# Gated delta rule: whole 128x128 products in the scan, and q's norm taken out of the products

## Chip, cores and metric

One core of a Trainium2 chip runs the whole program. The metric is the device time of one execution in microseconds (us): the median of several runs. One execution is also recorded by the hardware profiler, and every row below is from that record.

## What is computed

A network of two blocks of two layers each on 512 tokens of 1024 features, in float32. The change touches one part alone, the mixer of the second layer of the first block, a gated delta rule with 8 heads of 128. Its reference, cut to what matters:

```python
qkv = silu(causal_depthwise_conv(proj[..., :3 * 1024], conv_w))     # 4 taps
q = l2norm(q) * 128 ** -0.5;  k = l2norm(k)
decay = exp(where(incl, g[..., :, None] - g[..., None, :], -inf))   # chunks of 64 tokens
lower = where(strict, einsum('cd,sd->cs', k * beta, k) * decay, 0)
u, w  = solve(lower + eye, [v * beta, k * beta * exp(g)])
attn  = einsum('cd,sd->cs', q, k) * decay
def step(state, ...):                                                # 8 chunks, one after the other
    v_new = u_c - w_c @ state
    o     = (q_c * exp(g_c)) @ state + attn_c @ v_new
    state = state * exp(g_last) + (k_c * exp(g_last - g_c)).T @ v_new
o = rmsnorm(o, norm_g) * silu(z)
```

## The kernel before

The mixer is the method `gdn` (L811). A large product (L243 to L245) is done three times, in exact high and low parts, with 128 weight rows and 512 tokens each; it is called background below where it fills time between other steps. Per head there are these steps.

- `gdn_pre` (L948): the convolutions of k, q and v (`gdn_conv`, L909: a projection on TensorE, a copy by ScalarE, four taps on VectorE, a silu on ScalarE). k and then q are normed: squares on ScalarE, their sums by four products (L338), a power on GpSimd (L352), for q a factor on VectorE (L958), four transposes on TensorE that spread the result over the rows (L359), and a multiplication on VectorE into the tile `qk` (L960). Then the products of k with k and with q (L965), times the decay, give `U` and `at` (L969, L972); `wq`, `bk`, `kd` and `u` are prepared.
- `gdn_inverse` (L1000): a triangular inverse, first as a long chain of short VectorE instructions (L1016 to L1018), then as products on TensorE (L1027) with copies in between; it ends with the copies into `u` and `wq` (L1066).
- `gdn_scan` (L1068): eight steps in a chain, one for each chunk of 64 tokens. Two chunks share a tile of 128 partitions, and chunk e of a tile lies on partitions 64e to 64e+63. A step is a product of the state `S` with `wq` (L1079, 128 rows, 128 columns), a subtraction on VectorE into `vn` (L1082, 64 partitions), the product `at` by `vn` (L1083, 64 rows and 64 columns), the product `kd` by `vn` (L1087, 64 rows and 128 columns; not in the last step), the new `S` on VectorE (L1088) and a copy of the output by ScalarE (L1090). A float32 product is issued as two passes, so each counts twice in the rows.
- `gdn_out` (L1092): the norm of the output over its 128 features (squares, a sum, a factor and epsilon, L1098 and L1099, a power on GpSimd, L1101, a multiplication, L1102), four transposes, the gate and the split into parts. `out_proj` follows for pairs of heads.

The loop of `gdn` writes head after head: three heads' `gdn_pre` ahead, then for each head its scan, the inverse of the head after the next, `gdn_pre` of the third one on, the gate rows and the output. Heads 6 and 7 are scanned together at the end. The order on each engine is made from this program by a list scheduler when the kernel is built, from priorities and assumed durations; on the chip each engine takes its instructions in that order. So background products of later heads stand between the steps of a scan on TensorE.

Of the kernel before, what the change touches and what calls it, by code (L numbers as in the profile page):

```python
# [9 lines left out]
F32 = mybir.dt.float32  # L10
# [19 lines left out]
# ------------------------------------------------------------------ constants  # L30

class Pack:
    """Columns of a [128, n] array, by name."""
# [15 lines left out]
def shape_constants():  # L49
    """Arrays that depend on shapes alone: identity, masks, rope tables."""  # L50
# [4 lines left out]
    # causal mask, q on partitions  # L55
    c.add("causal", np.where(col <= row, 0.0, NEG))
    # stick-breaking, k on partitions and q along the free axis; the first 128
    # columns are the queries before the diagonal block
# [3 lines left out]
    # partial rope: per-row inverse frequency and sign of the sine  # L62
# [4 lines left out]
    # gated delta rule: 64-token chunks, two to a 128-token tile  # L67
# [10 lines left out]
    # axial rope, signed sines; dims 64 and 32  # L78
# [9 lines left out]
    # window attention: the blocks before and after the query's  # L88
# [6 lines left out]
def vector_packs(v):  # L95
    """Small vectors, features along partitions (layout only); the second pack
    is needed in the second block alone."""
# [18 lines left out]
# ------------------------------------------------------------------ kernel  # L116

# of the steps between the heads of a unit, the share spread evenly; the rest follows them
SPEED = 0.6
# of the convolutions, by unit: the stream that ends, the one that starts, steps of it;  # L120
# last, the steps before the first unit
CONV0 = (("", "", 3), ("", "", 3), ("c", "x", 4), ("", "", 8), ("x", "", 0), ("", "", 0), 4)
CONV1 = (("", "", 4), ("", "", 2), ("", "", 0), ("", "", 0), ("x", "", 0), ("", "", 0), 6)
# weights loaded ahead of the steps that take them
AHEAD = 2
# groups whose weights times values are float32 products, to spare the split
WHOLE_A, WHOLE_C, WHOLE_D = False, True, False
# background steps per product of 512 tokens with [1024, 128]; such products per pair of heads
# [4 lines left out]
class Step:  # L133
    """Something to do, and the (chunk, column) of the weights that it takes."""
# [5 lines left out]
class Net:  # L140
# [5 lines left out]
    # ---- small helpers  # L146
# [21 lines left out]
    def split(self, hi, lo, src, scale=None):  # L168
        """hi + lo = src exactly, hi with 12 significant bits."""
        nc = self.nc  # L170
        if scale is None:
            nc.scalar.copy(hi, src)  # L172
            nc.vector.tensor_sub(lo, src, hi.bitcast(F32))  # L173
        else:
            nc.scalar.mul(hi, src, scale)
            nc.vector.scalar_tensor_tensor(lo, src, scale, hi.bitcast(F32),
                                           op0=ALU.mult, op1=ALU.subtract)

    def exp_and_ln(self, after):
        """the activation tables that hold both, once `after` is there"""  # L180
# [4 lines left out]
    def tick(self, work):  # L185
        """background steps, so many per product of 512 tokens with [1024, 128]"""
# [11 lines left out]
    # ---- weights  # L198
    def wchunk(self, src, cut="col"):
        """Rows k*128.., columns -> get(k, c0, m): the exact (hi, lo) parts of a  # L200
        block. Loaded and split in units of 1024 when first used: all rows of
        some columns, or half of the rows."""
# [22 lines left out]
    def load_ahead(self, *uses):  # L225
        """steps that load weights, (src, column[, row, cut]) each, before their phase"""
# [12 lines left out]
    def mm3(self, out, terms):  # L239
        """out = sum of lhs^T rhs, each operand as (hi, lo)."""  # L240
# [6 lines left out]
    def mm_fm(self, out, w, c0, h, kt=KD, m=P):  # L247
        """Features on partitions: out[m, tokens]. The first ones after a norm go
        in two halves of the tokens, as these become ready."""
# [7 lines left out]
    def mm_tm(self, out, w, c0, n, h, t, kt=KD):  # L257
        """Tokens on partitions: out[128 tokens, n features]."""
# [3 lines left out]
    def t2(self, tag, n=T, dtype=F32, rows=P):  # L262
        """A short-lived [rows, n] tile, n <= 512. Tiles of one tag are given
        out in the order of the program, so steps of a chain have their own."""
# [6 lines left out]
    def psum_pool(self, **banks):  # L271
        """The half of PSUM that a phase cuts up for itself, into tags of so many
        banks (s: pairs of banks); the other half is dn and tp in all phases."""
# [13 lines left out]
    # ---- conditioning vectors  # L287
    def ada_tasks(self, w, groups, conds, dsts, bias, bufs=3, bank="st", on_pe=()):
        """conds[i] @ w + bias into dsts[i] ([128, 48], column j: features 128j..),
        as a list of steps of a quarter MB of weights each; on_pe: of the halves  # L290
        of groups, those that the tensor engine sums."""
# [34 lines left out]
    def gain_scale(self, dst, g, mod, grp):  # L326
        """dst = g * (1 + scale)"""
# [3 lines left out]
    # ---- norms  # L331
    def rstd_cols(self, acc, n, mat, scale=1.0, tag="rs"):
        """acc [128, n tokens] (sums of squares per partition), mat the averaging
        matrix (over scale) -> rstd per token, tokens on partitions [128, n/128]."""
# [7 lines left out]
    def rstd(self, means, nt, scale=1.0, tag="rs"):  # L342
        """(means scale + eps)^-1/2; scale: a number, or columns"""
# [11 lines left out]
    def bcast_rows(self, r, nt):  # L355
        """[128, nt] per-token values -> [128, nt*128] on all partitions (PSUM)."""
# [5 lines left out]
    def mean_squares(self, w, x, weights):  # L362
        """sums over the features of x^2 times weights(k) [128, j]: tokens on partitions, [128, n/128, j]"""
# [18 lines left out]
    def modulated(self, w, x, rb, A, B, hh, hl):  # L382
        """hh + hl = x * rb * A + B"""
# [12 lines left out]
    def norm_work(self):  # L396
        """short-lived tiles of a norm of 256 tokens: n and m one each, others in turn"""
# [12 lines left out]
    def hnorm(self, x, n, A, B, pool=None, size=256):  # L410
        """h = x * rstd * A + B in exact parts, and the steps that make it, two
        for `size` tokens: their norms, and the rest."""
# [21 lines left out]
    def normed_residual(self, x, n, g, A=None, B=None):  # L434
        """Steps, two for 256 tokens, for x = x * rstd * g in place; and, for A
# [1472 lines left out]
```

## Time and profile before

| | |
|---|---|
| runs | 3471.39 us median of 3 (3466.99 to 3474.49) |
| profiled execution, span from first to last instruction | 3467.6 us |
| mean granted TensorE clock | 0.980 |
| TensorE busy in the span | 3301.1 us (95%) |
| VectorE busy | 2207.0 us (64%) |
| ScalarE busy | 1274.4 us (37%) |
| GpSimd busy | 98.7 us (3%) |
| the delta rule's stage | from about 778 us to 1199 us of the span |

For the profiled execution the span is what is recorded; the time of a run also holds what lies before its first and after its last instruction, and the median of the runs is 3.8 us above that span. Products are pipelined, and the duration shown for one overlaps the next, so what a product costs TensorE is read from the distances between starts.

### The profile page before, as it was taken

Reading aid. Unit: us, or ns where it says so; the run is one execution under the profiler, and the core shown is the slowest. Engines: PE = TensorE matmul, PEld = TensorE weight load, DVE = VectorE, ACT = ScalarE, POOL = GpSimd, SP = SyncE. Lnnn points to the kernel's source line nnn. Section 1 sums busy time; section 2 is a strip of 40 time slices with the busy share of each in tenths; the row PEclk is TensorE's granted clock in tenths of the full one; section 3 lists DMA queues with packets and bytes.
Section 4 is the critical chain, followed back from the end, with each engine's and each line's share of the span. In section 5 each row is a group of like instructions: output and inputs, shape, how many; then the busy total and the mean of one; then the engine's idle time right before and its main releaser. Section 6 shows DMA issues by size and latency. Waiting matters only on the chain.

```text
span 3467.6 us, 47045 instructions
## 1 busy us (share of the span) xinstructions
PE 3301.1 (95%) x17888; PEld 2698.8 (78%) x17888; DVE 2207.0 (64%) x4501; ACT 1274.4 (37%) x2467; POOL 98.7 (3%) x122
## 2 busy tenths in 40 slices
PE   7998999999999999999899989999999898989999
PEld 4886888877777687887777768888888776778886
DVE  6977655568877576666777876543444976753334
ACT  3566322234433232223554453212122555442222
POOL 4000000000000000000000000000000000000000
PEclk9999999999999999999999999999999999989999
DMA  7554455532111155553443322333332443413332
GB/s 227 169 141 149 125 166 168 160 99 56 43 43 49 39 165 152 164 156 104 120 131 89 109 83 77 110 109 116 110 110 64 122 135 103 120 48 98 97 92 79
DMA packets 480082, 389.78 MB, mean 112 GB/s; under 512 B 21360, under 2 KB 390128, under 8 KB 479856
## 3 DMA queue, kind: packets, MB, share of 16 engines
q1 hardware_dynamic: 479856, 386.77, 37.4%
q8 instruction: 141, 2.31, 0.3%
q14 instruction: 85, 0.70, 0.1%
HBM read 356.28 MB, written 17.83 MB: 108 GB/s over the span
## 4 chain that ended last, share of the span: by engine, by line
PE 43%; DVE 4%; ACT 3%; issue 1%; DMA 1%; POOL 0%; SPq 0%; POOLq 0%; DVEq 0%; ACTq 0%
PE dn L243 6%; PE dn L244 6%; PE dn L245 6%; PE d L243 6%; PE d L245 6%; PE d L244 6%; PE tp L1181 1%; PE s L1217 1%; PE tp L1200 1%; PE tp L1207 1%; ACT pr L1160 1%; DVE cv L1346 1%; DVE wlo L173 1%; PE dn L370 1%; DVE st L1157 0%
## 5 line engine op out<-in xcount | busy, mean ns | idle before, releaser
L172 ACT CAST whi<-raw 128x1024 fp32r<-128x1024 f32 (+1 forms) x399 | 417.1, 1046 | 785.9 <-PE d L245 429.6
L173 DVE TENSOR_TENSOR wlo<-raw,whi 128x1024 fp32r<-128x1024 f32 (+1 forms) x399 | 486.5, 1220 | 284.0 <-ACT whi L172 283.7
L243 PE MATMUL dn<-hh,whi 128*128 128x512 f32 (+1 forms) x1688 | 620.8, 369 | 9.9 <-ACT t2b L1331 4.7
L244 PE MATMUL dn<-hh,wlo 128*128 128x512 f32 (+1 forms) x1688 | 614.6, 365 | 0.0
L245 PE MATMUL dn<-hl,whi 128*128 128x512 f32 (+1 forms) x1688 | 612.8, 364 | 0.0
L243 PE MATMUL d<-hh,whi 128*128 128x512 f32 (+1 forms) x1120 | 400.7, 358 | 0.0
L244 PE MATMUL d<-hh,wlo 128*128 128x512 f32 (+1 forms) x1120 | 399.9, 357 | 0.0
L245 PE MATMUL d<-hl,whi 128*128 128x512 f32 (+1 forms) x1120 | 399.8, 357 | 0.0
L243 PEld LDWEIGHTS dn<-hh,whi 128*128 128x128 f32 x1688 | 321.4, 191 | 60.6 <-ACT t2b L1331 5.3
L245 PEld LDWEIGHTS dn<-hl,whi 128*128 128x128 f32 x1688 | 320.8, 190 | 47.5 <-issue 2.9
L244 PEld LDWEIGHTS dn<-hh,wlo 128*128 128x128 f32 x1688 | 321.7, 191 | 43.8 <-issue 1.6
L310 DVE SCALAR_TENSOR_TENSOR acc<-araw,cond,acc 128x512 f32<-128x512 f32 x322 | 241.9, 751 | 67.1 <-DMA araw<-in_ada_w 39.0
L243 PE MATMUL d<-gh,whi 128*128 128x512 f32 (+1 forms) x696 | 251.6, 362 | 0.0
L244 PE MATMUL d<-gh,wlo 128*128 128x512 f32 (+1 forms) x696 | 249.9, 360 | 0.0
L245 PE MATMUL d<-gl,whi 128*128 128x512 f32 (+1 forms) x696 | 248.7, 360 | 0.0
L243 PEld LDWEIGHTS d<-hh,whi 128*128 128x128 f32 x1120 | 210.7, 188 | 32.6 <-issue 1.3
L244 PEld LDWEIGHTS d<-hh,wlo 128*128 128x128 f32 x1120 | 210.8, 188 | 32.5 <-issue 1.3
L245 PEld LDWEIGHTS d<-hl,whi 128*128 128x128 f32 x1120 | 210.7, 188 | 31.5 <-DVE hl L390 0.9
L243 PEld LDWEIGHTS d<-gh,whi 128*128 128x128 f32 x696 | 130.6, 188 | 26.4 <-issue 3.1
L245 PEld LDWEIGHTS d<-gl,whi 128*128 128x128 f32 x696 | 130.1, 188 | 24.6 <-issue 2.6
L244 PEld LDWEIGHTS d<-gh,wlo 128*128 128x128 f32 x696 | 130.6, 188 | 23.7 <-issue 2.2
L507 DVE TENSOR_TENSOR t2b<-t2a,d 128x512 f32<-128x512 f32 (+1 forms) x67 | 42.0, 627 | 154.4 <-PE d L245 154.3
(493 smaller groups left out, 5666.3 us busy)
## 6 DMA issues: line engine op xcount, KB each, us to landing
araw<-in_ada_w SPq DMA_DIRECT2D x192, 256.0 KB, 3.8
araw<-in_w_ada SPq DMA_DIRECT2D x192, 256.0 KB, 3.0
raw<-in_ffn_w_in SPq DMA_DIRECT2D x88, 512.0 KB, 4.0
raw<-in_ffn_w_out SPq DMA_DIRECT2D x44, 512.0 KB, 4.3
raw<-in_w_in SPq DMA_DIRECT2D x44, 512.0 KB, 3.9
raw<-in_w_gate SPq DMA_DIRECT2D x44, 512.0 KB, 3.7
raw<-in_w_up SPq DMA_DIRECT2D x44, 512.0 KB, 3.7
raw<-in_w_down SPq DMA_DIRECT2D x44, 512.0 KB, 3.8
```

What stands on the lines that cost most here:

```text
L172: nc.scalar.copy(hi, src)
L173: nc.vector.tensor_sub(lo, src, hi.bitcast(F32))
L243: self.nc.tensor.matmul(out, lhsT=lh, rhs=rh, start=j == 0, stop=False)
L244: self.nc.tensor.matmul(out, lhsT=ll, rhs=rh, start=False, stop=False)
L245: self.nc.tensor.matmul(out, lhsT=lh, rhs=rl, start=False, stop=j == n - 1)
L310: nc.vector.scalar_tensor_tensor(st[i], raw, s, st[i], op0=ALU.mult, op1=ALU.add)
L370: nc.tensor.matmul(sums, lhsT=weights(k), rhs=sq, start=k == 0, stop=k == KD - 1)
L507: nc.vector.tensor_mul(y, s, pu[:, :n])
L1160: nc.scalar.activation(pr, s, AF.Exp, bias=st[:, 0:1], accum_out=st[:, 2:3])
L1181: nc.tensor.transpose(tp[:, n * P:(n + 1) * P], pr[:, c:c + P], self.ident)
L1200: nc.tensor.matmul(ps[:64, q0:q1], lhsT=lhs, rhs=pt[sl // 2][0][:, sl % 2, q0:q1].bitcast(F32), start=j == 0, stop=j == nb - 1, skip_group ...
L1207: nc.tensor.matmul(ps[:, q0:q1], lhsT=lhs, rhs=pt[sl // 2][i][:, sl % 2, q0:q1], start=j == 0 and i == 0, stop=j == nb - 1 and i == 1, ski ...
```

## The change

The products `at` by `vn` and `kd` by `vn` take all 128 rows. For that `vn` has four fixed tiles, two for each half of the partitions, in which the other half is set to zero once, at the start; the subtraction still writes 64 partitions. The product with `at` also takes 128 columns: the tile `at_` has 64 more columns on either side, set to zero by GpSimd, and a window of 128 columns is chosen so that the chunk's 64 fall on the right half of the output; the other 64 add into rows of the bank that nobody reads afterwards. q is no longer normed ahead of the products: silu writes q straight into `qk`, and the norm's factor, one per token, is kept as `rq` and applied to the output at its norm: the mean square is multiplied by rq squared, and the result of the power by rq. The transposes and the multiplication that spread q's norm over the rows are gone. Comments are also left out of the file.

```diff
@@ gdn
+            self.vn = [[gp.tile([P, P], F32, name=f"vn{e}{i}") for i in range(2)] for e in range(2)]
+            self.vn_turn = [0, 0]
+            for tiles in self.vn:
+                for t in tiles:
+                    nc.gpsimd.memset(t, 0.0)
@@ gdn_conv(self, gp, w_in, tile_no, h, dst=None)
-        nc.scalar.activation(acc, acc, AF.Silu)
-        return acc
+        out = acc if dst is None else dst
+        nc.scalar.activation(out, acc if dst is None else acc.rearrange("p (t c) -> p t c", c=P), AF.Silu)
+        return out
@@ gdn_pre
-        for j in (1, 0):
-            q = self.gdn_conv(gp, w_in, j * 8 + hd, h)
-            sq = self.t2("b")
-            nc.scalar.activation(sq, q, AF.Square)
-            r = self.rstd_cols(sq, T, self.mean_d, float(D))
-            if j == 0:
-                nc.vector.tensor_scalar(r, r, 128.0 ** -0.5, None, op0=ALU.mult)
-            rb = self.bcast_rows(r, 4)
-            nc.vector.tensor_mul(qk[:, :, 1 - j, :], q.rearrange("p (t c) -> p t c", c=P),
-                                 rb.rearrange("p (t c) -> p t c", c=P))
+        k = self.gdn_conv(gp, w_in, 8 + hd, h)
+        sq = self.t2("b")
+        nc.scalar.activation(sq, k, AF.Square)
+        rb = self.bcast_rows(self.rstd_cols(sq, T, self.mean_d, float(D)), 4)
+        nc.vector.tensor_mul(qk[:, :, 0], k.rearrange("p (t c) -> p t c", c=P),
+                             rb.rearrange("p (t c) -> p t c", c=P))
+        q = self.gdn_conv(gp, w_in, hd, h, qk[:, :, 1])
+        sq = self.t2("b")
+        nc.scalar.activation(sq.rearrange("p (t c) -> p t c", c=P), q, AF.Square)
+        st["rq"] = gp.tile([P, 4], F32, tag="rq", bufs=4, name="rq")
+        nc.vector.tensor_scalar(st["rq"], self.rstd_cols(sq, T, self.mean_d, float(D)), 128.0 ** -0.5, None, op0=ALU.mult)
...
-        st["at"] = gp.tile([P, 4, P], F32, tag="at", bufs=4, name="at")
+        st["at_"] = gp.tile([P, 640], F32, tag="at", bufs=4, name="at")
+        nc.gpsimd.memset(st["at_"][:, :64], 0.0)
+        nc.gpsimd.memset(st["at_"][:, 576:], 0.0)
+        st["at"] = st["at_"][:, 64:576].rearrange("p (t c) -> p t c", c=P)
@@ gdn_scan
-                vn = gp.tile([P, P], F32, tag="vn", bufs=4, name="vn")
+                self.vn_turn[e] ^= 1
+                vn = self.vn[e][self.vn_turn[e]]
                 nc.vector.tensor_sub(vn[r], st["u"][r, t], ps[r, :P])
-                nc.tensor.matmul(ps[q, :P], lhsT=st["at"][r, t, 64 * e:64 * e + 64], rhs=vn[r],
+                c0 = t * P + P * e
+                nc.tensor.matmul(ps[:, :P], lhsT=st["at_"][:, c0:c0 + P], rhs=vn,
                                  start=False, stop=True, skip_group_check=True)
                 if n < 7:
                     pu = ps[:, P:]
-                    nc.tensor.matmul(pu[:, :P], lhsT=st["kd"][r, t], rhs=vn[r], start=True, stop=True)
+                    nc.tensor.matmul(pu[:, :P], lhsT=st["kd"][:, t], rhs=vn, start=True, stop=True)
@@ gdn_out
+        rq2 = gp.tile([P, 4], F32, tag="rq2", bufs=2, name="rq2")
         nc.vector.tensor_reduce(r, sq, axis=AX.X, op=ALU.add)
-        nc.vector.tensor_scalar(r, r, 1.0 / 128, EPS, op0=ALU.mult, op1=ALU.add)
+        nc.vector.scalar_tensor_tensor(rq2, st["rq"], 1.0 / 128, st["rq"], op0=ALU.mult, op1=ALU.mult)
+        nc.vector.tensor_mul(r, r, rq2)
+        nc.vector.tensor_scalar(r, r, EPS, None, op0=ALU.add)
         r2 = self.sp.tile([P, 4], F32, tag="go_r", bufs=2, name="go_r")
         nc.gpsimd.tensor_tensor(out=r2, in0=r, in1=self.mhalf[:, :4], op=ALU.pow)
+        nc.vector.tensor_mul(r2, r2, st["rq"])
```

## Rows read from the trace of the kernel before

**Rows 1.** The page's busy times: engine, busy us, share, instructions.
```profile
PE 3301.1 (95%) x17888; PEld 2698.8 (78%) x17888; DVE 2207.0 (64%) x4501; ACT 1274.4 (37%) x2467; POOL 98.7 (3%) x122
```

**Rows 2.** Windows over the delta rule: length, busy us per engine, clock, DMA share, GB/s.
```profile
857.00:898.00 41.00, 40.82 (x240) 32.22 (x238) 35.88 (x134) 18.55 (x32) 3.70 (x6) 1.00 0.15 40
898.00:945.00 47.00, 45.83 (x257) 36.51 (x258) 41.82 (x158) 19.94 (x34) 4.23 (x6) 1.00 0.16 45
945.00:1015.00 70.00, 65.89 (x372) 53.32 (x371) 51.74 (x144) 22.91 (x38) 3.82 (x6) 0.98 0.17 46
1015.00:1065.00 50.00, 48.64 (x269) 37.70 (x269) 43.39 (x148) 19.74 (x34) 4.24 (x6) 1.00 0.15 43
1065.00:1122.00 57.00, 55.08 (x294) 42.86 (x294) 42.22 (x113) 20.12 (x33) 4.00 (x4) 1.00 0.22 56
1122.00:1147.00 25.00, 25.00 (x118) 17.06 (x116) 19.83 (x85) 6.93 (x16) 0.00 (x0) 1.00 0.22 69
1187.00:1199.00 12.00, 6.23 (x23) 4.71 (x24) 6.83 (x14) 2.62 (x6) 2.01 (x2) 0.58 0.15 46
```

**Rows 3.** TensorE's timeline: one scan step of head 5, and two state products in a row.
```profile
1140.12 0.40 PE L245 MATMUL dn<-hl,whi 128*128 128x512 f32 x1
1140.45 0.43 PE L1083 MATMUL c<-vn,at 64*64 64x128 f32 x2
1140.81 0.48 PE L1087 MATMUL c<-vn,kdec 64*128 64x128 f32 x2
1141.22 0.50 PE L243 MATMUL dn<-hh,whi 128*128 128x512 f32 x1
1141.56 0.40 PE L244 MATMUL dn<-hh,wlo 128*128 128x512 f32 x1
1141.80 0.39 PE L245 MATMUL dn<-hl,whi 128*128 128x512 f32 x1
1142.03 0.61 PE L1079 MATMUL c<-S,wq 128*128 128x128 f32 x4
1142.39 0.47 PE L243 MATMUL dn<-hh,whi 128*128 128x512 f32 x1
1142.70 0.39 PE L244 MATMUL dn<-hh,wlo 128*128 128x512 f32 x1
```

**Rows 4.** VectorE's timeline in that step: the subtraction into vn.
```profile
1139.86 0.28 DVE L1082 TENSOR_TENSOR vn<-uv,c 64x128 f32<-64x128 f32 x1
```

**Rows 5.** Waits in the stage, 780 to 1200: who waited for whom, us, times, longest.
```profile
PEld c L1083 <- DVE vn L1082: 8.6, 17, 1.2
```

**Rows 6.** Weight loads of the products with at and wq: ns min/median/max, first and last start.
```profile
L1079 PEld LDWEIGHTS c<-S,wq x128: 186/188/330, 857.4 to 1186.3; 128*128 128x128 f32 x128
L1083 PEld LDWEIGHTS c<-vn,at x128: 129/131/133, 858.7 to 1187.4; 64*64 64x64 f32 x128
```

**Rows 7.** TensorE's timeline: the transposes of q's norm in head 0.
```profile
796.39 0.62 PE L359 MATMUL tp<-c_ident,rs_r 128*128 128x128 f32 x4 [0.94 <-DVE rs_r L958]
796.76 0.48 PE L243 MATMUL dn<-hh,whi 128*128 128x512 f32 x1
797.08 0.40 PE L244 MATMUL dn<-hh,wlo 128*128 128x512 f32 x1
```

**Rows 8.** Groups by line, 778 to 1199: busy us, mean ns, idle before, its releasers.
```profile
L359 PE MATMUL tp<-c_ident,rs_r 128*128 128x128 f32 x64 | 10.5, 282 | 10.3 <-DVE rs_r L958 5.1 <-POOL rs_r L352 4.4 <-DVE W L1017 0.7
L960 DVE TENSOR_TENSOR qk<-t2a,tp 128x512 f32<-128x512 f32 x16 | 10.9, 683 | 5.4 <-PE tp L359 3.4 <-ACT whi L172 1.9
```

**Rows 9.** VectorE's timeline at the end of the stage, in the output's norm.
```profile
1188.09 0.17 DVE L1099 TENSOR_SCALAR go_v<-go_v 128x4 f32<-128x4 f32 x1
1189.45 0.69 DVE L1102 TENSOR_TENSOR o<-o,go_r 128x512 f32<-128x512 f32 x1 [1.19 <-POOL go_r L1101]
```

**Rows 10.** An inverse with little beside it: its first wide step, and the product after it.
```profile
1145.65 0.69 DVE L1032 TENSOR_TENSOR Rf<-R,c_blk 128x512 f32<-128x512 f32 x1
1159.67 0.71 PE L1079 MATMUL c<-S,wq 128*128 128x128 f32 x4 [0.24 <-ACT wq L1066]
```

More of the change, by code (lines that the diff above doesn't have):

```diff
@@ L907, in gdn, with gdn_conv @@
             output(3)
-    def gdn_conv(self, gp, w_in, tile_no, h):
+    def gdn_conv(self, gp, w_in, tile_no, h, dst=None):
         nc = self.nc
```

## The prediction

> **What bounds the kernel now.** I read the page's busy times first: TensorE is busy for 95% of the span, the next engine, VectorE, for 64% [rows 1]. That is a mean over stages, so the next view is the windows over the delta rule alone. In the scans TensorE's busy time fills almost the whole of each window, but VectorE is no longer far behind: 35.88 of 41, 41.82 of 47 and 43.39 of 50 us in the scans of heads 0, 1 and 3, against 0.74 to 0.79 of the other windows before 1147 [rows 2]. So here TensorE sets the time with VectorE close by. Overlapping durations make "busy" a poor measure of TensorE; the third view is therefore its timeline, where the distance from start to start says what an instruction costs.
>
> That timeline shows the point of the whole case [rows 3]. Undisturbed background products start 0.235 us apart (1141.56, 1141.80, 1142.03). Around `at` and `kd` the distances grow: 0.33 from the background product to `at`, 0.36 to `kd`, 0.41 to the next background product, and 0.34 to the one after it. The subtraction that gives `vn` began at 1139.86 and took 0.28 [rows 4]; it was done at 1140.14, 0.31 us before `at` began, so in this step the wait for data isn't what makes the distances long. Right behind stand two state products in a row, with 128 rows and 128 columns each and four passes in all, the same count as `at` and `kd`. They push the stream far less [rows 3].
>
> **The two scan products.** From 1140.12 to 1141.56 are 1.44 us; two background distances in them are 0.47, so `at` and `kd` cost 0.97 us. From 1141.80 to 1142.70 are 0.90 us; less the same 0.47, four whole passes cost 0.43. The difference is 0.54 us per step. The changed products have just the form of the cheap ones, and their stationary operands (`at_`, `kdec`) are ready long before, as `wq` is. There are 8 heads with 7 steps that have both products: 56 x 0.54 = 30.2 us. The eighth step has `at` alone: 0.095 too much ahead of it, 0.36 for it and 0.105 too much behind make 0.56; half of the four passes is 0.215; 8 x 0.35 = 2.8. Together 33.0 us.
>
> Not all of this is there to be gained. In 17 of the 64 steps the weight load of `at` waits for `vn` [rows 5]. In these the extra 0.095 us ahead of `at` lies inside the wait and stays: 17 x 0.095 = 1.6. Left are 31.4 us. The bounds: 33.0 if the wait shortens too, and nothing, or less, if shape isn't the cause (the first rival).
>
> Weight loads are what speaks against the change. That of `at` takes 131 ns with 64 columns, that of `wq` 188 with 128 [rows 6]: the new `at` loads 57 ns more in each of 128 passes, 7.3 us in all where nothing hides it. The four whole passes above already hold four loads of 128 columns, so the 0.43 contains this. The Trainium skill, TensorE: Matmul & The Clock Gate, in its closing table and under LDWEIGHTS, says that a single product with few rows takes the same time as one with 128, and that a weight load's time goes by its columns and not by its rows. By that rule `kd` gains nothing, `at` gets dearer, and this part would be a loss of at most the 7.3 us above instead of a gain of 31.4; the two loads agree with it, the distances of the timeline do not [rows 3, 6]. I take the distances, since they are what the stream pays.
>
> **q's norm.** The four transposes go, on TensorE and for each head: from 796.39 to 797.08 are 0.69 us, less one background distance 0.455 [rows 7]; 8 x 0.455 = 3.6 us. Ahead of the transposes TensorE stood idle: 5.1 us of the group's idle time were ended by the factor on VectorE (L958), which belongs to q [rows 8]. The rest, 4.4 us ended by GpSimd, is k's, which stays. Afterwards the products in `qk` wait for q's silu alone. The squares, four sums, power and factor of q are still done, but TensorE does not wait for their result. I take 4.0 of the 5.1, since some of the stall can come back at the next thing TensorE wants; the bounds are 0 and 5.1.
>
> On VectorE the multiplication by q's norm goes, 8 of 0.683 = 5.5 us [rows 8]. Three small instructions per head are new in the output's norm, at 0.17 like the one that stands there now [rows 9]: 24 x 0.17 = 4.1. The net 1.4 us is nothing beside the limit treated below. In the middle of the stage the new three are covered by background products. After the last scan they are not: between 1187 and 1199 TensorE is busy for 6.23 of 12 us at a granted clock of 0.58 of full speed [rows 2], waiting for this very chain twice, for heads 6 and 7. Two of the three, with some 0.2 us each from start to start, stand between the sum and the multiplication, and `rq2` can be made early; two heads give 0.8, and I put 1.0 us for the loss. Bounds: 0.4 (one head's chain hidden behind the other's) and 2.0 (all three in both, and the clock staying at half for longer).
>
> **Edits at nothing.** The zeroing of four `vn` tiles, once, and of two borders per head goes to GpSimd, which is busy for 98.7 us of 3467.6 [rows 1] and for 0 to 4.24 us of each window above [rows 2]. If one came late, the multiplication into `at` would wait, and behind it on VectorE all that follows; it needs only the buffer of a head whose scan is over, so I price it at nothing, with a bound of 0.5 us for each of 8 heads. q's silu now needs `qk`, of which there is one buffer; but k's multiplication, earlier in the same head, needs it already.
>
> **The limit by VectorE.** In the three dense windows are 138 us, of them 121.1 with VectorE busy (0.88) [rows 2]. TensorE would save there 21 x 0.54 + 3 x 0.35, less half of the 1.6 for waits, 11.6, and for three heads of q's norm 3 x 0.95 = 2.9, in all 14.5 us. The rest, 123.5 us, would have VectorE busy for 98%. An engine that waits at every step for TensorE will hardly reach that. Between 0.88 (all 14.5 lost) and 1 (nothing lost) I take 0.94: 128.8 us, so 9.2 are gained and 5.3 lost.
>
> **Sum.** 31.4 + 3.6 + 4.0 - 1.0 - 5.3 = 32.7 us less. The stages behind are only shifted. The profiled span is 3467.6 us and the median of the runs 3471.4; the same difference taken from the median gives 3438.7, so 3439 us.
>
> **Rivals.** *Shape isn't the cause.* Were the long distances those of two dependent products behind a fresh `vn`, they would stay. For it speak the 17 waits [rows 5]; against it the 0.31 us between `vn` and `at` in the step shown, and that `kd`, which waits for nothing new, starts only 0.36 behind `at` [rows 3, 4]. Then only the q part is left, 7.6 less 1.0, and up to 7.3 us of dearer weight loads go against it: 3471.4 - 6.6 + 7.3 = 3472, no change. This is also what the skill's rule on rows and columns would give. Chance 0.08.
>
> *VectorE becomes the bound.* If it gets no denser than 0.88 in the three windows, 14.5 us are lost there, and if the lag spreads to the neighbouring ones, some 5 to 8 more: 38.0 - 14.5 - 6.5 = 17 us less, 3454. For it speaks VectorE's share [rows 2]; against it that VectorE now often waits for TensorE, time that shrinks by itself. Chance 0.20.
>
> *Slower: inverses lose their cover.* The schedule is made anew, with fewer instructions in it. An inverse with little beside it took from 1145.65 to 1159.67, 14.0 us [rows 10]; its own products on TensorE, six groups of eight passes and four transposes, are 52 passes at 0.11 [rows 3], 5.7 us; 8.3 us of it need background products to fill them. If the new order spends these earlier, each inverse left bare costs 8.3. From four bare inverses on (33.2) the gain is gone; with five the time is 3471.4 - 32.7 + 41.5 = 3480. For it: the order is a scheduler's, and a bare one is seen above. Against it: the amount of background work is the same. Chance 0.06.
>
> **How the numbers follow.** The forecast has 0.57, with a range of its own of 3430 to 3448 (4.0 and 1.6 us more from waits, all of VectorE's 5.3; or no stall saved and 5 us more lost to VectorE). A larger gain, from a luckier order on top of all upper bounds, 3424 to 3430, has 0.09. With VectorE as bound down to 11 us of gain (3461) the range is 3424 to 3461; outside are the first and the third rival and a few hundredths at either end. Faster by over 0.2% (7 us, about what a measurement of this kernel can tell from no change): 0.57 + 0.20 + 0.09 = 0.86; within it 0.08; slower 0.06.
>
> **What would show it.** In the timeline of the changed kernel, `at` should start 0.23 us behind the background product, and `at` with `kd` push the stream by 0.43. The transposes of L359's group should be 32 passes in place of 64, and its idle time about 5 us shorter. The first `at` at 858.7 and the last at 1187.4 [rows 6] should stand some 27 to 30 us closer. VectorE's share in the dense windows should be near 0.94. I am wrong if the distances around `at` and `kd` stay, if TensorE gets as many new waits for `vn` and for the state as distances have shrunk, or if gaps of 8 us open in the inverses.

## The result, and the profile after

The changed kernel takes 3445.31 us (median of 4 runs, 3443.76 to 3451.82), the kernel before in runs of the same chip 3470.62 (3466.99 to 3474.49): a ratio of 0.9927 [0.9915, 0.9938], 25.3 us less. The forecast was 3439.

The shares of busy time on the page don't move ([rows 1] are those of before), as TensorE's busy time and the span shrink together:

```profile
PE 3273.7 (95%) x17856; PEld 2692.6 (78%) x17856; DVE 2202.9 (64%) x4517; ACT 1274.1 (37%) x2467; POOL 98.8 (3%) x142
```

So I use marks. The last power of a norm on GpSimd ahead of the delta rule, and the first one behind it, are the same instructions in every kernel of this study; the distance between their starts is called the stage below. First GpSimd's timeline of before, then of after (start, duration):

```profile
763.07 0.87 POOL L352 TENSOR_TENSOR rs_r<-rs_v,mhalf 128x2 f32<-128x2 f32 x1 [13.61 <-DVE rs_v L348]
...
1210.14 0.70 POOL L352 TENSOR_TENSOR rs_r<-rs_v,mhalf 128x2 f32<-128x2 f32 x1 [16.82 <-DVE rs_v L348]
```

```profile
765.04 0.86 POOL L352 TENSOR_TENSOR rs_r<-rs_v,mhalf 128x2 f32<-128x2 f32 x1 [8.14 <-DVE rs_v L348]
...
1182.49 0.70 POOL L352 TENSOR_TENSOR rs_r<-rs_v,mhalf 128x2 f32<-128x2 f32 x1 [16.14 <-DVE rs_v L348]
```

The stage shrinks from 447.07 to 417.45 us, by 29.6. The spans differ by only 25.6 (3467.6 and 3442.0). The missing 4 us lie ahead of the first mark and behind the last, where the program is the same but for some zeroing on GpSimd. Over the fourteen profiles of this study that part takes 3018.5 to 3026.6 us: 3020.5 before, 3024.5 in the changed kernel and 3022.6 when that was profiled once more, but also 3023.4 and 3024.4 in two kernels without the zeroing (e6 and e2 below). So it is scatter. The stage is therefore the sharper measure, and a second series of runs of the changed kernel (below) gave 417.38 for it again, with 28.2 us less in the medians.

What answers to [rows 3] is TensorE's timeline of one scan step of the changed kernel:

```profile
1117.13 0.40 PE L245 MATMUL dn<-hl,whi 128*128 128x512 f32 x1
1117.37 0.38 PE L1098 MATMUL c<-vn,at 128*128 128x128 f32 x2
1117.59 0.39 PE L1102 MATMUL c<-vn,kdec 128*128 128x128 f32 x2
1117.73 0.48 PE L243 MATMUL dn<-hh,whi 128*128 128x512 f32 x1
1118.05 0.40 PE L244 MATMUL dn<-hh,wlo 128*128 128x512 f32 x1
```

The four distances are 0.24, 0.22, 0.14 and 0.32, together 0.92; less two background distances (0.47) the pair costs 0.45 us, where it cost 0.97. The forecast for a whole pair was 0.43.

The weight load of `at` is 57 ns longer, as forecast (131 ns in [rows 6]), and the pair is cheaper all the same:

```profile
L1098 PEld LDWEIGHTS c<-vn,at x128: 186/188/192, 855.3 to 1158.6; 128*128 128x128 f32 x128
```

The groups by line, 770 to 1185 us (busy us, mean ns | idle before, its releasers), show q's transposes gone, 32 passes of L359 where [rows 8] have 64:

```profile
L359 PE MATMUL tp<-c_ident,rs_r 128*128 128x128 f32 x32 | 5.3, 284 | 7.0 <-POOL rs_r L352 4.4 <-POOL pad L920 2.6
...
L987 PE MATMUL tp<-c_ident,beta 128*128 128x128 f32 x32 | 4.9, 276 | 3.1 <-DVE U L984 2.0 <-DVE W L1028 1.1
```

The wait for q's factor is gone with them. But TensorE's waits between the marks (us in total, times, longest) now name others:

```profile
PE tp L359 <- POOL rs_r L352: 4.7, 6, 1.6
PE i L1124 <- DVE o L1121: 4.4, 2, 4.0
PE tp L359 <- POOL pad L920: 2.6, 2, 1.7
PE dn L243 <- ACT yh L172: 2.6, 2, 1.5
PE i L1039 <- DVE Tm L1070: 2.5, 2, 1.7
PE tp L987 <- DVE U L984: 2.0, 4, 0.7
...
PE tp L987 <- DVE W L1028: 1.1, 1, 1.1
```

For comparison, rows of the same view of the kernel before. The first two have no successor above; the last two, the tail of the stage, have:

```profile
PE tp L359 <- DVE rs_r L958: 5.1, 6, 1.3
...
PE c L1083 <- DVE vn L1082: 3.3, 6, 1.1
PE i L1105 <- DVE o L1102: 2.7, 2, 2.4
PE dn L243 <- ACT yh L172: 2.3, 2, 1.5
```

Gone are 5.1 for q's factor and 3.3 for `vn`, 8.4 together. New are 2.6 ahead of k's transposes, 3.1 ahead of the transposes of beta (L987), 2.0 in an inverse (`Tm`, 2.5, against 0.5 before) and 1.7 at the tail (`o`), 9.4 together. All such waits between the marks add up to 22.1 us before and 22.8 after. The name `pad` is not the true releaser: GpSimd's timeline has k's power directly ahead of that 0.10 us memset, and the power is what is late (the transposes start at 815.28, 0.054 us behind its end, as they do behind every power that holds them up):

```profile
813.73 1.50 POOL L352 TENSOR_TENSOR rs_r<-rs_v,mhalf 128x4 f32<-128x4 f32 x1 [6.95 <-DVE rs_v L348]
815.18 0.10 POOL L920 MEMSET pad<- 128x4 f32 x1
```

That view shows idle time of over 0.15 us behind the end of a product, and as durations overlap, smaller delays don't stand in it. One kind of them is new. In the step shown above, VectorE's update of the state `S` ends at 1118.50, and the next state product, due 0.23 us behind the background product at 1118.28, starts only at 1118.65. In the kernel before the update of the step in [rows 3] was done at 1141.68, 0.35 us ahead of the next state products (1142.03). Two rows of after, one of before:

```profile
1118.16 0.34 DVE L1103 SCALAR_TENSOR_TENSOR S<-S,last,c 128x128 f32<-128x128 f32 x1
1118.65 0.46 PE L1091 MATMUL c<-S,wq 128*128 128x128 f32 x2
...
1141.33 0.35 DVE L1088 SCALAR_TENSOR_TENSOR S<-S,last,c 128x128 f32<-128x128 f32 x1 [0.30 <-PE c L1087]
```

In the changed kernel the next state product starts within 0.15 us of the end of the update in 23 of the 56 steps that have one, in the kernel before in 3.

### The profile page after: what moved, and what is told of

Read it like the earlier page. It is cut to its first block, busy times and chain, and to the rows that moved or that the text cites. A ratio compares the mean times of both kernels' runs of the same rounds, so it can differ in the third digit from the quotient of the medians.

```text
span 3442.0 us, 47012 instructions
## 1 busy us (share of the span) xinstructions
PE 3273.7 (95%) x17856; PEld 2692.6 (78%) x17856; DVE 2202.9 (64%) x4517; ACT 1274.1 (37%) x2467; POOL 98.8 (3%) x142
## 4 chain that ended last, share of the span: by engine, by line
PE 43%; DVE 4%; ACT 3%; issue 1%; DMA 1%; POOL 0%; POOLq 0%; DVEq 0%; SPq 0%; ACTq 0%
PE dn L243 6%; PE dn L244 6%; PE dn L245 6%; PE d L243 6%; PE d L244 6%; PE d L245 6%; PE tp L1200 1%; PE s L1236 1%; PE tp L1219 1%; PE tp L1226 1%; ACT pr L1179 1%; DVE cv L1365 1%; DVE wlo L173 1%; PE dn L370 1%; DVE ptl L173 0%
## 5 line engine op out<-in xcount | busy, mean ns | idle before, releaser
L244 PEld LDWEIGHTS d<-hh,wlo 128*128 128x128 f32 x1120 | 210.7, 188 | 32.3 <-issue 1.3
L245 PEld LDWEIGHTS d<-gl,whi 128*128 128x128 f32 x696 | 130.1, 188 | 24.6 <-issue 2.6
```

The costliest lines, as they stand in the source:

```text
L244: self.nc.tensor.matmul(out, lhsT=ll, rhs=rh, start=False, stop=False)
L245: self.nc.tensor.matmul(out, lhsT=lh, rhs=rl, start=False, stop=j == n - 1)
```

## The experiments

Three explanations were tested against each other. *Shape*: a product whose form (its rows and weight columns) differs from its neighbours' costs the stream something at every change of form. *Rows and columns*: only rows count, or, by the rule weighed in the prediction, rows cost nothing and columns go by their load. *VectorE*: what was missing from the forecast was lost to VectorE's load. Then, whether the two parts of the change add up, and whether a better version exists. "Before" is always the kernel before on the same chip.

| kernel | median us | before | ratio | stage us |
|---|---|---|---|---|
| before | | | | 447.07 |
| the changed kernel | 3445.31 | 3470.62 | 0.9927 [0.9915, 0.9938] | 417.45 |
| e4_kd_64_rows | 3456.00 | 3470.30 | 0.9959 [0.9944, 0.9974] | 432.78 |
| e9_both_64_rows | 3454.02 | 3470.30 | 0.9957 [0.9940, 0.9973] | 430.06 |
| e3_at_64_columns | 3459.04 | 3470.30 | 0.9967 [0.9954, 0.9980] | 432.74 |
| e5_at_64_64 | 3458.44 | 3470.30 | 0.9963 [0.9948, 0.9977] | 432.02 |
| e1_scan_only | 3446.23 | 3473.09 | 0.9926 [0.9911, 0.9942] | 421.35 |
| e2_norm_only | 3467.50 | 3473.09 | 0.9984 [0.9974, 0.9993] | 440.96 |
| e6_before_two_taps | 3471.09 | 3473.09 | 0.9997 [0.9988, 1.0007] | 444.92 |
| e7_after_two_taps | 3439.61 | 3473.09 | 0.9909 [0.9890, 0.9927] | 415.56 |
| c1_after_again | 3442.82 | 3471.05 | 0.9923 [0.9911, 0.9935] | 417.38 |
| c2_scan_only_again | 3446.46 | 3471.05 | 0.9930 [0.9918, 0.9942] | 420.03 |
| e8_eps_over_q | 3435.39 | 3471.05 | 0.9900 [0.9887, 0.9913] | 409.71 |
| e10_eps_and_beta_bank | 3453.90 | 3471.05 | 0.9952 [0.9940, 0.9964] | 424.87 |

**`kd` with 64 rows again.** One line of the changed kernel; the order on every engine stays that of the changed kernel.

```diff
-   nc.tensor.matmul(pu[:, :P], lhsT=st["kd"][:, t], rhs=vn, start=True, stop=True)
+   nc.tensor.matmul(pu[:, :P], lhsT=st["kd"][r, t], rhs=vn[r], start=True, stop=True)
```

> The changed kernel with the product of kd back on 64 rows; the order on every engine is the changed kernel's. Theory 1 (each change of the products' shape on TensorE, rows or columns, is paid where it happens): some 0.1 us more ahead of kd, 0.2 in it and 0.1 behind it, 0.39 x 56 = 22 us slower than the changed kernel. Theory 2 (only an unequal number of rows is paid): the same 22 us. Rule of columns (a product on 64 rows costs what one on 128 does): no change, within 3 us.

TensorE's timeline of the same step:

```profile
1117.64 0.40 PE L244 MATMUL dn<-hh,wlo 128*128 128x512 f32 x1
1117.88 0.39 PE L1098 MATMUL c<-vn,at 128*128 128x128 f32 x2
1118.19 0.48 PE L1102 MATMUL c<-vn,kdec 64*128 64x128 f32 x2
1118.61 0.50 PE L245 MATMUL dn<-hl,whi 128*128 128x512 f32 x1
1118.95 0.40 PE L243 MATMUL dn<-hh,whi 128*128 128x512 f32 x1
```

The distances are 0.24, 0.31, 0.42 and 0.34: 1.31 less 0.47 is 0.84, so that 64 empty rows save 0.39 us of this step. The stage grows by 15.3 us over 56 such products, 0.27 for each, where 22 were expected. That rows cost nothing is refuted. That the mean is 0.7 of the single step's price matters below.

**Both products with 64 rows** (128 columns each, again in the same order).

```diff
-   nc.tensor.matmul(ps[:, :P], lhsT=st["at_"][:, c0:c0 + P], rhs=vn,
+   nc.tensor.matmul(ps[:, :P], lhsT=st["at_"][r, c0:c0 + P], rhs=vn[r],
```

and the line of `kd` as above.

> The changed kernel with at and kd both on 64 rows and 128 columns, same order on every engine. Theories 1 and 2: the change of shape ahead of at and the one behind kd are paid, none between them: 0.85 us for the pair in place of 0.45, 56 x 0.40 + 8 x 0.35 = 25 us slower than the changed kernel, so nearly the kernel before. Rule of columns: no change, within 3 us.

The same step has 0.33, 0.32, 0.32 and 0.33 (starts 1118.08, 1118.41, 1118.73, 1119.05 and 1119.38): 0.83 for the pair. One product of 64 rows or two in a row cost the same. So it is entering and leaving the other form that is paid, not each small product. The stage grows by 12.6 us, half of the 25 expected and less than with `kd` alone. Part of the reason stands in the last two heads, which are scanned together, one a step ahead of the other, so that their products lie on opposite halves of the partitions. In six of these steps the products of 64 rows run side by side, their passes starting two by two 13 to 14 ns apart, and eight passes take 0.65 us. From the background product ahead of them to the second one behind are 1.31 us, as against 1.36 in the changed kernel and 2.13 with `kd` alone on 64 rows:

```profile
1148.23 0.50 PE L1098 MATMUL c<-vn,at 64*128 64x128 f32 x4
1148.56 0.40 PE L1102 MATMUL c<-vn,kdec 64*128 64x128 f32 x4
1148.88 0.50 PE L244 MATMUL dn<-yh,wlo 128*128 128x512 f32 x1
```

**`at` with 64 columns, at 128 rows and at 64.**

```diff
-   nc.tensor.matmul(ps[:, :P], lhsT=st["at_"][:, c0:c0 + P], rhs=vn,
+   nc.tensor.matmul(ps[q, :P], lhsT=st["at"][:, t, 64 * e:64 * e + 64], rhs=vn,
```

and in the second kernel

```diff
-   nc.tensor.matmul(ps[:, :P], lhsT=st["at_"][:, c0:c0 + P], rhs=vn,
+   nc.tensor.matmul(ps[q, :P], lhsT=st["at"][r, t, 64 * e:64 * e + 64], rhs=vn[r],
```

> The changed kernel with at on 128 rows but 64 columns, kd whole. Theory 1: 0.1 us more ahead of at and 0.14 more between at and kd, 56 x 0.23 + 8 x 0.35 = 16 us slower than the changed kernel. Theory 2: not slower, up to 7 us faster by the shorter weight load. Rule of columns: the same as theory 2.

> The changed kernel with at on 64 rows and 64 columns as before, kd whole; the order on every engine is that of the run with 64 columns. Theories 1 and 2: 16 us slower than the changed kernel; against the run with 64 columns, theory 1: the same, theory 2: 16 to 23 us slower. Rule of columns: not slower than the changed kernel.

TensorE's timeline of one step at 128 rows and 64 columns:

```profile
1122.68 0.40 PE L245 MATMUL dn<-hl,whi 128*128 128x512 f32 x1
1123.00 0.43 PE L1097 MATMUL c<-vn,at 128*64 128x128 f32 x2
1123.37 0.49 PE L1101 MATMUL c<-vn,kdec 128*128 128x128 f32 x2
1123.61 0.48 PE L243 MATMUL dn<-hh,whi 128*128 128x512 f32 x1
1123.92 0.40 PE L244 MATMUL dn<-hh,wlo 128*128 128x512 f32 x1
```

The pair costs 1.24 - 0.47 = 0.77; at 64 rows and 64 columns (starts 1123.54, 1123.87, 1124.23, 1124.47, 1124.79) 0.78. The two kernels have the same order as each other (another than the changed kernel's), and stages of 432.74 and 432.02, 15.3 and 14.6 us above the changed kernel's where 16 were expected. Columns alone are thus as dear as rows and columns together, and fewer columns with their shorter weight load are no help. For `at` both halves of the padding, rows and columns, are needed.

**Each part alone.** The first is the changed kernel with `gdn_pre` and `gdn_out` of before, the second the kernel before with `gdn_pre` and `gdn_out` of the changed one (the scan's lines as before).

> The whole products of the scan alone; q's norm stays ahead of the products as before. By the sum of the prediction: 31.4 us less 4 to 5 for VectorE, 27 us faster than before (3443). Rival (a third of what TensorE saves per step goes into new waits, as the run with kd on 64 rows hints, where 22 us by the steps' prices were 15 in the stage): 0.7 x 33 = 22 us, 3448.

> q's norm moved into the output's norm alone; the scan's products as before. By the sum of the prediction: 3.6 for the transposes and 4.0 for the stall, less 1.0 at the end of the stage, 6.6 us faster than before (3464). Rival (the stall comes back at the next thing TensorE waits for, and a new order costs as much as it brings): 0 to 3 us faster.

The scan's part takes 26.9 us in the medians (27 expected) and 25.7 in the stage; q's part 5.6 (6.6 expected) and 6.1. Together they would be 31.8 in the stage; the changed kernel has 29.6. To see how much of q's part is left on top of the scan's, both were run again on one chip, with no edit of their own:

> The changed kernel once more, beside the next three on one chip. If what lies outside the delta rule's stage is chance, the time before the stage and behind it differs from the first profile by up to 3 us either way, and the stage by less than 1 us from 417.5. If the 4 us outside the stage belong to the change, they stand there again.

> The scan's whole products alone, once more on the same chip. If moving q's norm adds to the gain (the stage of the profiles: 4 us), this is some 4 us slower than the changed kernel. If it adds nothing, since the stall comes back at other products, both are within 2 us.

3446.46 against 3442.82: q's part on top is worth 3.6 us in the medians; in the stage 3.9 (421.35 to 417.45) and 2.6 (420.03 to 417.38) in the two pairs.

**Less for VectorE to do.** Two of the four taps of the convolutions are left out, in the kernel before and in the changed one, so these two compute another convolution.

```diff
-        for j in range(1, 4):
+        for j in range(1, 2):
```

> The kernel before with two of the four taps of every convolution in the delta rule left out (its result is not the reference's): 48 instructions of 0.745 us, 35.8 us, less on VectorE. If TensorE alone sets the stage before, it gets hardly faster: 0 to 5 us, by shorter chains in front of k and q. If VectorE sets it in part: over 8 us.

> The changed kernel with the same two taps left out. Theory (VectorE eats part of the gain): the distance to the run of the kernel before with two taps grows from 29.6 us in the stage to the full sum on TensorE, 36 to 39 us. Rival (the rest of the gain goes to something else, such as the order or the inverses' chains): the distance stays at 28 to 32 us.

In the changed kernel the groups by line, 855 to 1165 us, give one tap 744 ns:

```profile
L926 DVE SCALAR_TENSOR_TENSOR t2a<-pad,vec,t2a 128x512 f32<-128x512 f32 x45 | 33.5, 744 | 0.3
```

Left out are 2 taps of 3 convolutions of 8 heads, 48 x 0.744 = 35.7 us of instructions. As these overlap others, VectorE's busy time between the marks falls by less, by 24.6 us before (347.0 to 322.4) and by 24.5 after (343.0 to 318.5). The stage shrinks by 2.1 us in the kernel before and by 1.9 in the changed one, and the distance between them stays, 29.4 against 29.6 us. The medians differ by 31.5 us, but they hold the scatter outside the stage. Were the missing gain lost to VectorE's load, it would have come back here. As far as the load goes, that explanation falls; of VectorE's place in the chain of a step it says nothing.

**Epsilon over q's norm.** The output's norm is (sum/128 x rq^2 + eps)^-1/2 x rq, which is (sum/128 + eps/rq^2)^-1/2. As rq is itself a power of a sum, eps/rq^2 is 128 eps (sum of q's squares + eps), linear in the sum: no power on GpSimd and no factor for q, and two instructions less on VectorE between sum and multiplication at the output.

```diff
-        st["rq"] = gp.tile([P, 4], F32, tag="rq", bufs=4, name="rq")
-        nc.vector.tensor_scalar(st["rq"], self.rstd_cols(sq, T, self.mean_d, float(D)), 128.0 ** -0.5, None, op0=ALU.mult)
+        sums = self.psum("st")
+        for t in range(4):
+            nc.tensor.matmul(sums[:, t * P:(t + 1) * P], lhsT=sq[:, t * P:(t + 1) * P], rhs=self.mean_d,
+                             start=True, stop=True)
+        st["eq"] = gp.tile([P, 4], F32, tag="rq", bufs=4, name="eq")
+        nc.vector.tensor_scalar(st["eq"], sums.rearrange("p (t q) -> p t q", q=P)[:, :, 0], 128.0 * EPS * D,
+                                128.0 * EPS * EPS, op0=ALU.mult, op1=ALU.add)
@@ gdn_out
-        nc.vector.scalar_tensor_tensor(rq2, st["rq"], 1.0 / 128, st["rq"], op0=ALU.mult, op1=ALU.mult)
-        nc.vector.tensor_mul(r, r, rq2)
-        nc.vector.tensor_scalar(r, r, EPS, None, op0=ALU.add)
+        nc.vector.scalar_tensor_tensor(r, r, 1.0 / 128, st["eq"], op0=ALU.mult, op1=ALU.add)
...
-        nc.vector.tensor_mul(r2, r2, st["rq"])
```

> The changed kernel without q's power and without the factor: epsilon over rq squared is linear in q's sum of squares, so one VectorE instruction makes it from the sums, and the output's norm has its old length of one instruction before the power and none behind it. If the end of the stage and the small instructions cost what the prediction said (1.0 us at the end, 24 instructions of 0.17 beside other work): 1 to 2 us faster than the changed kernel. If GpSimd's powers hold up k's transposes (7.0 us of waits): 3 to 5 us faster.

This version beats both kernels: 3435.39 us, 7.4 below the changed kernel on the same chip, more than either expectation had; the stage is 7.7 shorter. TensorE's waits in it:

```profile
PE tp L359 <- POOL rs_r L352: 5.4, 7, 1.6
PE dn L243 <- ACT yh L172: 2.9, 2, 2.0
PE i L1125 <- DVE o L1122: 2.2, 2, 1.9
PE tp L359 <- POOL pad L920: 1.7, 1, 1.7
PE i L1044 <- DVE Tm L1075: 0.9, 1, 0.9
```

The waits ahead of beta's transposes have no row any more, the inverse's went from 2.5 to 0.9 and the tail's for `o` from 4.4 to 2.2; that for `yh`, also of the tail, is 2.9 where it was 2.6. Ahead of k's transposes it is still 7.1 us (7.3 in the changed kernel), so the reason that I had named for a large gain, GpSimd's powers in front of them, isn't the one. All waits between the marks add up to 15.0 us, 7.8 less than in the changed kernel, and the stage is 7.7 shorter. Whether the shorter chains or the order that the scheduler made anew took them away was not separated.

**Beta's transposes in another bank.** On top of the last: they took turns in a bank with other short products, and were to use that of the inverses.

```diff
-        br = self.psum("p")
+        br = self.psum("i")
```

> The same with the transposes of beta in a bank of the inverse's pair, in place of the pair that U is read from. If the stall of q's norm came back there because the pair was full (waits of 3.1 us for U): these waits go, up to 3 us faster than the run without q's power. If the order matters more than the bank: within 2 us of it, or slower where the inverse now waits for its bank.

It loses 15.2 us of stage and 18.5 in the median. The wait that it was to remove had gone already with the last edit, so there was nothing to win. What it cost is spread: the summed waits rise to 25.6 us, by 10.6, and stand in 38 places instead of 18. Among the largest grown or new rows are these:

```profile
PE tp L359 <- POOL rs_r L352: 7.6, 8, 1.4
PE i L1125 <- DVE o L1122: 5.0, 2, 4.1
PE c L1096 <- DVE S L1108: 1.4, 3, 0.9
```

Whether the shared bank itself or the order that the scheduler then made is at fault was not separated.

## Why the prediction was right, and where it was off

The time lies in the forecast's own range (3430 to 3448), 6.6 us above the forecast itself. In the sharper measure, the stage, 29.6 us of the 32.7 forecast were gained.

**Shape: the mechanism holds.** The pair fell from 0.97 to 0.45 us in the step that is shown (forecast 0.43), and the four kernels with one part of the padding undone stand between, at 0.77 to 0.84. They tell more than the prediction had: columns alone cost as much as rows with columns, and two small products in a row no more than one. By these rows the price is one of changing the form of the product. The step before has three changes of form and pays 0.52 us for them; the four kernels have two each and pay 0.32 to 0.39. The Trainium skill, TensorEngine Tiling (Array Packing), Key Properties, says that a change of tiling mode drains TensorE. These rows agree with it, at about 0.3 to 0.4 us of stream for one excursion. The rule that was weighed against the change (the Trainium skill, TensorE: Matmul & The Clock Gate, closing table and LDWEIGHTS) agrees with the loads alone (131 to 188 ns); of the distances it would have given the opposite sign, and the first rival fell with it.

**An account of the stage.** To see where each term of the sum went, I took TensorE's starts between the marks, pass by pass, and set each distance against the one that is usual there: 0.232 us for a pass of 512 columns, 0.120 for 256, 0.111 for the others. (A pass of 512 behind a shorter one is shown 0.08 us early, which is why `kd` above is followed after 0.14 and the next product after 0.32; that is put right.) What is over is counted under `at` and `kd`, from the pass ahead of them to the second one behind them; under waits, as the waits view has them; or under the rest. This is an estimate to about 1 us.

| us | usual distances | at `at` and `kd` | waits | rest | stage |
|---|---|---|---|---|---|
| before | 369.3 | 32.3 | 22.1 | 23.4 | 447.1 |
| e1_scan_only | 369.3 | 2.9 | 20.5 | 28.7 | 421.4 |
| e2_norm_only | 365.8 | 31.2 | 21.8 | 22.2 | 441.0 |
| the changed kernel | 365.8 | 1.8 | 22.8 | 27.1 | 417.4 |
| e4_kd_64_rows | 365.8 | 22.7 | 21.6 | 22.7 | 432.8 |
| e8_eps_over_q | 365.8 | 2.2 | 15.0 | 26.7 | 409.7 |

**31.4 us for the scan's products and 3.6 for the transposes: right.** At `at` and `kd` 30.5 us went, and 3.5 with the passes of the transposes. The price read from one step holds nearly everywhere: behind `kd` it is paid whether a background product follows or, as in 20 steps, another of 128 columns (it starts 0.20 in place of 0.11 behind, and the pass after it 0.21 in place of 0.11). The 1.6 us taken off for waits for `vn` were meant for time that would stay in such waits; `at`'s loads waited 8.6 us in 17 places [rows 5] and now wait 1.4 in 6, so there it didn't stay. An estimate to 1 us can't tell 31.4 from 33.0.

**The step that failed: 4.0 of the stall's 5.1.** The stall ahead of q's transposes did go, but the sum of the waits went from 22.1 to 22.8 us: it came back ahead of k's own transposes, of beta's, in an inverse and at the tail. I had written that "some of the stall can come back at the next thing TensorE wants", and put that at 1.1; all of it did. It came back with q's part alone too: 21.8 us of waits. That run's 5.6 us in the medians and 6.1 in the stage come near the forecast of 3.6 + 4.0 - 1.0 = 6.6, but not by the stall: 3.5 are the transposes, and the other 2.6 are spread over the other columns of the table, where order and scatter can't be told apart. On top of the scan's part it brings 2.6 to 3.9, about what the transposes alone are. The version with epsilon over q's norm shows from the other side that such waits are real time: it has 7.8 us less of them and is 7.7 us faster in the stage.

**The limit by VectorE: 5.3 us, near in size, for a wrong reason.** The rest grew by 3.7 us, so something of that size did limit the gain. VectorE's share did rise, in windows of the lengths of [rows 2] about the scans of heads 0, 1 and 3:

```profile
855.00:896.00 41.00, 38.42 (x234) 32.03 (x234) 37.08 (x155) 18.11 (x31) 4.16 (x8) 1.00 0.15 39
896.00:943.00 47.00, 44.64 (x278) 37.10 (x277) 43.14 (x157) 18.67 (x32) 3.99 (x7) 1.00 0.16 46
1010.00:1060.00 50.00, 47.94 (x274) 39.42 (x273) 44.28 (x151) 20.57 (x34) 4.07 (x8) 1.00 0.20 54
```

124.5 of 138 us are 0.90, between the 0.88 of before and the 0.94 expected. But with the lighter convolutions VectorE is busy for 0.77 of the changed kernel's stage, as it is before the change (0.78; 0.82 in the changed kernel), and the gain was no larger. What limits is the chain of a step: state product, subtraction, `kd`, update of `S`, next state product. The delays ahead of the state products that show no idle time, all counted in the rest, add up to 0.7 us before, 4.8 in the changed kernel and 4.8 in its second profile, and to 0.5 in the kernel with `kd` on 64 rows, whose order is that of the changed kernel. The state product starts within 0.15 us of the end of the update in 3, 23, 22 and 4 of the 56 steps of these. So where the products around it get shorter, TensorE arrives at the next state product before the state does, and this is why 20.9 us of distances, put back by `kd` on 64 rows, moved the stage by 15.3 only. The prediction had named new waits for the state as a sign of being wrong; they came, in a small part. VectorE has a hand in the chain: in the median the update started 0.04 us behind the end of `kd` before and 0.22 after. With the lighter convolutions it is 0.04 again, yet 31 of the 56 state products start within 0.15 us, so the chain limits without VectorE's other work too. That the term came out near is luck.

**Where in the stage.** The first `at` of each head shows it. From the first mark to head 3's scan the stretch went from 252.5 to 241.3 us, by 11.2, where three scans, six heads' transposes and the stall promised 12.4 + 2.7 + 4.0 = 19.1; from there to the last mark from 194.5 to 176.2, by 18.3, where five scans, two heads' transposes and the tail promised 20.7 + 0.9 - 1.0 = 20.6. The shortfall is in the early, dense part, and there most of it is the stall: by the same account 11.5 and 2.4 us came of the first two terms, and the waits grew by 1.2. With the lighter convolutions that part differs by 13.3 us (253.9 and 240.6), 2.1 more. So VectorE's load explains at most about a quarter of what is missing there. The order, which the scheduler makes anew, was not held fixed between before and after.

**The signs.** The first and the last `at` stand 25.5 us closer, where 27 to 30 were named, and the idle time of L359's group is 3.3 us shorter (10.3 to 7.0), where about 5 were.

**Two sums of the prediction are off.** The lower end of the range takes 4.0 us more from waits where only 1.1 of the 5.1 were left; 1.1 + 1.6 + 5.3 give 3431, so the bound hardly moves. An inverse has seven groups of eight passes, not six: 60 passes, 6.6 us, so that 7.4 and not 8.3 us of it would be bare.

**The tail: 1.0 us expected, 1.2 measured.** From the last `at` to the last mark are 22.75 us before and 23.92 after. VectorE's timeline there shows why it is more than the added instructions:

```profile
1159.05 0.16 DVE L1116 TENSOR_TENSOR go_v<-go_v,rq 128x4 f32<-128x4 f32 x1
1159.25 0.75 DVE L528 SCALAR_TENSOR_TENSOR x<-dn,mod,x 128x512 f32<-128x512 f32 x1
1159.91 0.16 DVE L1117 TENSOR_SCALAR go_v<-go_v 128x4 f32<-128x4 f32 x1
1161.20 0.16 DVE L1120 TENSOR_TENSOR go_r<-go_r,rq 128x4 f32<-128x4 f32 x1 [1.12 <-POOL go_r L1119]
1161.28 1.22 DVE L173 TENSOR_TENSOR wlo<-raw,whi 128x1024 fp32r<-128x1024 f32 x1
1162.42 0.68 DVE L1121 TENSOR_TENSOR o<-o,go_r 128x512 f32<-128x512 f32 x1
```

A residual of 0.75 us slipped between the two new instructions of 0.16, and a weight split of 1.22 us between the last small one and the multiplication that TensorE waits for. That wait is 4.0 us, against 2.4 before. Here each additional link in the chain was one more place where the order could put something long.

**The edits at nothing** cost nothing that can be seen: the borders' memsets take 0.15 us each on GpSimd. No inverse lost its cover by 8 us: TensorE's waits for `Tm` and `Rf` in the inverses are 3.8 us in all.

## What to carry to other kernels

Where a stream of whole products is broken by a small one, read the distances of starts around it, not its duration: here padding with zeros, more arithmetic and longer weight loads, saved 26 of 3470 us, and for the smaller product it needed rows and columns both. Count the changes of form, not the small products. Expect only part of the saving to arrive where a chain of steps runs beside the stream: here the state was then late in 23 of 56 steps, delays too short for the view of waits, so read the distance from the end of the producer to the start of the product. A stall that is removed should be followed to the next thing that its engine waits for: moving q's norm left the sum of the waits as it was, and the version with shorter chains lowered it.

## What the runs showed of the hardware that was not expected

- A product of 128 rows and 64 columns between whole ones costs as much extra (pair 0.77 us) as one of 64 and 64 (0.78), or one or two of 64 rows and 128 columns (0.84 and 0.83); all whole 0.45.
- By the single passes of the trace (the rows merge two), the first pass of a new form starts about 0.09 us late and the second one again, by 0.10 us with 128 weight columns and by 0.05 with 64. This holds on entering, between two small forms, and on going back to whole products.
- Products of 64 rows on opposite halves of the partitions ran side by side, with starts 13 to 14 ns apart: eight passes and the background products beside them took 1.31 us, no more than with eight whole passes (1.36).
- Where the state product followed closely on VectorE's update that it needs, it started as a rule 0.146 us behind the end of that (13 of the 23 close cases of the changed kernel lie between 0.145 and 0.147).
- A load of 128 float32 columns takes 57 ns longer than one of 64 and none of it showed in the stream.
- A power on 128x4 elements on GpSimd takes 1.0 to 1.6 us in the norms of q and k.
